# Interleaving the upper and lower halves of the weights column by column in one buffer

## The chip, the cores and the metric

The kernel runs on one core of one Trainium2 chip. The metric is the device time of one execution in microseconds (us). The core has five engines that run side by side and wait for each other through semaphores: TensorE (PE in the profile, with PEld for its weight loads), VectorE (DVE), ScalarE (ACT), GpSimd (POOL) and SyncE (SP, which issues the DMAs here). A matrix product on PE has two operands in SBUF: a stationary one of 128 x 128, which a weight load brings in, and a moving one, which a pass streams through the array. The result goes to PSUM. In the profile one pass is a MATMUL and the load ahead of it an LDWEIGHTS.

## The reference

Two pre-norm residual layers on x (256 tokens, 2,048 channels), float32 throughout:

```
h = rmsnorm(x, layer_norm[0]); y, gate = mla_mixer(h, ...)        # layer 0
x = x + (y * silu(gate)) @ mla_w_out
h = rmsnorm(x, layer_norm[1]); y, gate = swa_mixer(h, ...)        # layer 1
x = x + (y * silu(gate)) @ swa_w_out
return rmsnorm(x, final_norm)
```

Layer 0 is latent attention: h @ w_in gives a query latent and a key/value latent of 512 channels each, a rope key of 64 and a gate of 2,048; the latents are normed and projected up to 16 heads, and attention is causal. Layer 1 is sliding-window attention (window 128) with 32 query heads, 4 key/value heads and a sink logit per head. Almost all of the arithmetic is products of 256 tokens with weight matrices, 116 MB of weights in all.

## The kernel before

**Numbers in two halves.** A product in float32 is made of three passes in the format float32r. Each operand is split: `hi` is the value rounded to float32r, `lo` the rest. `proj` (lines 257 to 263) then adds hi x hi (line 261), hi x lo (262) and lo x hi (263) into one PSUM bank; in all three the weights (`wh`, `wl`) are stationary, 128 x 128, and the activations move, 128 x 256: `rhs[:, 0, :]` is their upper half, `rhs[:, 1, :]` their lower.

**Where the weights come from.** The class `Weights` keeps the list of all weight pieces, mostly 1,024 columns of 128 partitions, in the order of use. `load` fetches a piece by DMA into one of five raw buffers (`wraw`), three pieces ahead of the split. `split` makes the halves, two pieces ahead of use: ACT copies the piece into `whi` (line 93), DVE subtracts that from the raw piece into `wlo` (line 94). There are four pairs of such tiles, used in turn (`b` is 0 to 3), and `next` hands out a pair. One piece, the weights of the rope key (`w_kr`), goes through the other branch (lines 86 to 91), in which halves stand beside each other in blocks of 64 columns.

**Who uses them.** `slab` multiplies one piece of 1,024 columns with eight tiles of activations: 8 x 3 = 24 passes. Two slabs make 128 output channels. `hs0` to `hs15` are the normed input of a layer, `ys0` to `ys15` the gated output of the mixer, `cq` and `ck` the latents; each such tile has two halves of 256 columns (2,048 bytes a partition). Lines 530 to 532 (values of layer 0) and 613 to 615 (values of layer 1) are the other way round: activations are stationary and the weights move. Lines 738 and 745 do the last two output channels' blocks, with the lower halves of the weights first.

**Stages.** The input projection of layer 0 (16 pieces with eight banks open), eight groups of two heads, the output projection into x with 32 slabs on `ys`, the keys and values of layer 1, then 16 columns of sliding-window attention (loop over `c`: two slabs of query projection, two of gate, the scores of the next column, the products with the values), and the second output projection on `ys`. Within an engine the instructions run in the order in which a scheduler of the framework puts them; it follows the program's order and its own estimate of when operands come free. It also makes the waits, by the bytes that two instructions share, and the wait for a buffer by the tile: whoever writes a tile first in its next use waits for the last reader of its previous use.

**Where the tiles lie.** A tile of a pool lies behind the one that was made before. The four pairs of weight tiles have 4,160 and 4,096 bytes a partition, since `HI` puts 64 unused bytes ahead of each upper half. Taken modulo 256 bytes, the halves of pairs 0, 1, 2, 3 begin at 64, 128, 192 and 0 in the built program (both halves of a pair alike). `hs` begins at 0, `ys` at 0 and the latents at 32; `gap1` and `gap2` are tiles that nobody reads, which move what lies behind them.

Of the kernel before, what the change touches and what calls it, by code (L numbers as in the profile page):

```python
# [18 lines left out]
F32 = mybir.dt.float32  # L19
F32R = mybir.dt.float32r  # L20
# [5 lines left out]
P = 128  # L26
# [15 lines left out]
SUB = 1024  # L42
XQ = 4
WARM = 2

HI = [64, 64, 64, 64]
LO = [0, 0, 0, 0]
MASK_MLA = [(i + 16) % 32 for i in range(32)]
MASK_SWA = [i + 8 if i < 8 else i - 8 if i < 16 else i for i in range(32)]

# [1 line left out]
class Weights:  # L52
# [24 lines left out]
    def split(self, upto):  # L77
        while self.done < min(upto, len(self.pieces)):
            self.load(self.done + 1 + self.ahead_load)
            src, (_, n, beside) = self.raw.pop(self.done), self.pieces[self.done]  # L80
            self.done += 1
            b = (self.done - 1) % self.sub_bufs
            hi = self.pool.tile([P, SUB + HI[b] // 4], F32R, tag=f"whi{b}", name="whi", bufs=1)[:, HI[b] // 4:][:, 0:n]
            lo = self.pool.tile([P, SUB + LO[b] // 4], F32R, tag=f"wlo{b}", name="wlo", bufs=1)[:, LO[b] // 4:][:, 0:n]
            if beside:
                for i, t in enumerate((hi, lo)):
                    t = t.rearrange("p (k a c) -> p k a c", a=2, c=beside)
                    part = src[:, i * n // 2:(i + 1) * n // 2].rearrange("p (k c) -> p k c", c=beside)
                    self.nc.scalar.copy(out=t[:, :, 0, :], in_=part)
                    self.nc.vector.tensor_tensor(out=t[:, :, 1, :], in0=part, in1=t[:, :, 0, :].bitcast(F32),  # L90
                                                 op=ALU.subtract)
            else:
                self.nc.scalar.copy(out=hi, in_=src)  # L93
                self.nc.vector.tensor_tensor(out=lo, in0=src, in1=hi.bitcast(F32), op=ALU.subtract)  # L94
            self.ready.append((hi, lo))
# [8 lines left out]
def trunk(ctx: ExitStack, tc: tile.TileContext, a: dict):  # L104
# [3 lines left out]
    const = ctx.enter_context(tc.tile_pool(name="const", bufs=1))  # L108
# [9 lines left out]
    w = Weights(nc, wpool, raw_bufs=5, sub_bufs=4, ahead_load=3, ahead_split=2)  # L118
# [73 lines left out]


    hs = [const.tile([P, 2, S], F32R, name=f"hs{c}") for c in range(KC)]
    const.tile([P, 64], F32, name="gap1")
    ys = [const.tile([P, 2, S], F32R, name=f"ys{c}") for c in range(KC)]
    const.tile([P, 72], F32, name="gap2")


    def tiny(name, n=2, bufs=2):  # L200
# [196 lines left out]
    for k in range(KC):  # L397
        if k in (1, 3, 6):
            i = (1, 3, 6).index(k) + 1
# [6 lines left out]
        if k == 0:  # L406
            for half in range(2):
                hi, lo = w.next()
# [4 lines left out]
        elif k < KC - 2:  # L413
            hi, lo = w.next()
            for c in range(2 * RC):
                n = slice(c * P, (c + 1) * P)
                proj(acc[c], (hi[:, n], lo[:, n]), hs[k], False, False)
            sq_x.add(xc(k - 1))
        elif k == KC - 1:
# [3 lines left out]
            for c in range(2 * RC):  # L423
                n = slice(c * P, (c + 1) * P)
# [27 lines left out]
    def mix(g, vt, pt, sgs):  # L452

        (vh, vl, v1), (pth, ptl, pt1) = vt, pt
        yp = bank(ps_y, "yp")
        for j in range(2):
            v = slice(j * VD, (j + 1) * VD)
            n = slice(j * S, (j + 1) * S)
            o = yp[:, n]
            mm(o, lhsT=vh[:, v], rhs=pth[:, n], start=True, stop=False)  # L460
            mm(o, lhsT=vl[:, v], rhs=pth[:, n], start=False, stop=False)
            mm(o, lhsT=vh[:, v], rhs=ptl[:, n], start=False, stop=False)
            mm(o[:, P:], lhsT=v1[:, v], rhs=pt1[:, j * P:(j + 1) * P], start=False, stop=True)
        for j in range(2):
            n = slice(j * S, (j + 1) * S)
            yg = work.tile([P, S], F32, tag="yg", name="yg", bufs=2)
            dve.tensor_tensor(out=yg, in0=yp[:, n], in1=sgs[j], op=ALU.mult)
            split(ys[2 * g + j], yg)

    mixes = None  # L470
    for g in range(HEADS // 2):

        ps = bank(ps_p, "pp")
        hi, lo = w.next()
# [15 lines left out]
        if g == 0:  # L490
            t = bank(ps_y, "yp")
            tot = [q.total(t[:, 4 * i:4 * i + 4]) for i, q in enumerate((sq_x, sq_c["q"], sq_c["k"]))]
            r0 = rsqrt("r0", tot[0], D)

            sqc = rsqrt("sqc", tot[1], RANK, r0)
            nsq = small.tile([P, 2], F32, name="nsq")
            dve.tensor_tensor(out=nsq, in0=sqc, in1=r0, op=ALU.mult)
            dve.tensor_scalar(out=nsq, in0=nsq, scalar1=-MLA_SCALE, scalar2=None, op0=ALU.mult)
            skc = rsqrt("skc", tot[2], RANK, r0)
            sk = small.tile([P, 2], F32, name="sk")  # L500
            dve.tensor_tensor(out=sk, in0=skc, in1=r0, op=ALU.mult)
            t = bank(ps_y, "yp")
            r0B = row("r0B", r0, t[:, 0:S])
            skB = row("skB", sk, t[:, S:])
            ps = bank(ps_s, "sc")[:, 0:S]
            mm(ps, lhsT=fold, rhs=krn, start=True, stop=True)
            kr = work.tile([P, S], F32, tag="ro3", name="ro3")
            rope(kr, ps, cos0, sin0, MASK_MLA)
            dve.tensor_tensor(out=kr, in0=kr, in1=r0B, op=ALU.mult)
            split(krs, kr)  # L510

        ps = bank(ps_p, "pp")
        hi, lo = w.next()
# [10 lines left out]
        hi, lo = w.next()  # L524
        for i in range(2):
            t = slice(i * P, (i + 1) * P)
            for k in range(RC):
                n = slice(k * S, (k + 1) * S)
# [77 lines left out]
    for q in range(4):  # L606
        hi, lo = w.next()
        for i in range(2):
            t = slice(i * P, (i + 1) * P)
            for k in range(4):  # L610
                kk = 4 * q + k
                n = slice(k * S, (k + 1) * S)
# [79 lines left out]
    def gated(c):  # L692
        yg = work.tile([P, S], F32, tag="yg", name="yg", bufs=2)
        dve.tensor_tensor(out=yg, in0=y_of.pop(c), in1=sg_of.pop(c), op=ALU.mult)
        split(ys[c], yg)
# [37 lines left out]
    for c in tail:  # L733
        last[c] = [w.next(), w.next()]
        ps = bank(ps_p, "pp")[:, 0:S]
        for k in range(KC):
            n = slice(k % (KC // 2) * P, (k % (KC // 2) + 1) * P)
# [3 lines left out]
    def chunk(c, t):  # L741
        ps = bank(ps_p, "pp")[:, 0:S].rearrange("p (a q) -> p a q", a=2)
        for k in range(KC):
            n = slice(k % (KC // 2) * P, (k % (KC // 2) + 1) * P)
            mm(ps, lhsT=last[c][k // (KC // 2)][0][:, n], rhs=ys[k][:, :, t], start=k == 0, stop=k == KC - 1)  # L745
        xl = xc(c)[:, t]
        for n in range(2):
            dve.tensor_tensor(out=xl, in0=ps[:, n, :], in1=xl, op=ALU.add)
        sq = work.tile([P, P], F32, tag=("hx", "yg")[c % 2], name="sql", bufs=2)
        act.activation(out=sq, in_=xl, func=AF.Square)  # L750
        return sq
# [13 lines left out]
    def scaled(i, t, r2):  # L765
        r2B = bank(ps_s, "sc")[:, 0:P]
        mm(r2B, lhsT=r2[:, 0:1].to_broadcast([P, P]), rhs=ident, start=True, stop=True)
        r2B = r2B.rearrange("p (a q) -> p a q", a=1)
        for n in range(KC // XQ):
            for h in range(0, XQ, 2):  # L770
                o = x_t[n][:, h:h + 2, t]
                dve.tensor_tensor(out=o, in0=o, in1=r2B.to_broadcast([P, 2, P]), op=ALU.mult)  # L772
                if n == 0:
                    nc.sync.dma_start(out=a["out"][i, n][:, h:h + 2, :], in_=o)
            if n > 0:
                nc.sync.dma_start(out=a["out"][i, n], in_=x_t[n][:, :, t])
# [3 lines left out]
    sq = chunk(KC - 2, t1)  # L780
    r2 = norm(t0, parts)
    parts = [sq, chunk(KC - 1, t1)]
    const.tile([P, 120], F32, name="rest")
    scaled(0, t0, r2)
    scaled(1, t1, norm(t1, parts))

# [80 lines left out]
```

## Time and profile before

| | |
|---|---|
| median of 2 runs | 697.21 us (697.18 to 697.25) |
| the profiled execution: time, span | 696.82 us, 695.0 us |
| granted TensorE clock in it | 0.995 |
| PE, DVE, ACT, POOL busy | 681.6, 533.9, 428.0, 66.4 us |
| weight traffic | 117.00 MB, mean 168 GB/s |

The span runs from the first to the last instruction of the profiled execution. A pass is listed as 0.28 us long, but passes overlap in the pipeline: what counts is the time from the start of one to the start of the next. In a row of the groups, `pp<-hs,whi` names the output and the inputs, then come the shape, the count, the busy time and the mean length in ns of one, and behind the bar the idle time of the engine just before them and what ended it. The lines that the argument needs stand in the prediction.

### The profile page before, as it was taken

Reading aid. Unit: us, or ns where it says so; the run is one execution under the profiler, and the core shown is the slowest. Engines: PE = TensorE matmul, PEld = TensorE weight load, DVE = VectorE, ACT = ScalarE, POOL = GpSimd, SP = SyncE. Lnnn points to the kernel's source line nnn. Section 1 sums busy time; section 2 is a strip of 40 time slices with the busy share of each in tenths; the row PEclk is TensorE's granted clock in tenths of the full one; section 3 lists DMA queues with packets and bytes.
Section 4 is the critical chain, followed back from the end, with each engine's and each line's share of the span. In section 5 each row is a group of like instructions: output and inputs, shape, how many; then the busy total and the mean of one; then the engine's idle time right before and its main releaser. Section 6 shows DMA issues by size and latency. Waiting matters only on the chain.

```text
span 695.0 us, 14550 instructions
## 1 busy us (share of the span) xinstructions
PE 681.6 (98%) x5718; PEld 677.7 (98%) x5718; DVE 533.9 (77%) x1085; ACT 428.0 (62%) x853; POOL 66.4 (10%) x72
## 2 busy tenths in 40 slices
PE   8999999999999999999999999999999999999994
PEld 7999999999999999999999999999999999999994
DVE  5887787687688686666658899998998998766664
ACT  6666756666666665444446687687778768544430
POOL 3534000000000000111110000000000000022220
PEclk9999999999999999999999999999999999999998
DMA  8674554554554455555555544545445454455614
GB/s 311 243 223 143 167 164 139 170 166 142 174 164 144 162 174 162 193 182 190 182 183 171 165 156 152 171 149 162 157 149 165 152 168 153 153 185 187 191 45 122
DMA packets 37301, 117.00 MB, mean 168 GB/s; under 512 B 4208, under 2 KB 8944, under 8 KB 37232
## 3 DMA queue, kind: packets, MB, share of 16 engines
q1 hardware_dynamic: 37232, 116.06, 51.7%
q8 instruction: 45, 0.74, 0.4%
q14 instruction: 24, 0.20, 0.1%
HBM read 113.95 MB, written 2.10 MB: 167 GB/s over the span
## 4 chain that ended last, share of the span: by engine, by line
PE 89%; DVE 3%; ACT 3%; POOL 2%; issue 1%; DMA 1%; SPq 0%; DVEq 0%; ACTq 0%; POOLq 0%
PE pp L262 24%; PE pp L261 24%; PE pp L263 24%; PE pt L353 1%; ACT whi L93 1%; PE pp L745 1%; PE yp L680 1%; PE pp L532 1%; PE pp L530 1%; PE pp L531 1%; DMA wraw<-in_w_c 1%; DVE wlo L94 1%; POOL sq_x L227 1%; PE pt L354 1%; DVE x L772 1%
## 5 line engine op out<-in xcount | busy, mean ns | idle before, releaser
L93 ACT CAST whi<-wraw 128x1024 fp32r<-128x1024 f32 (+1 forms) x217 | 222.7, 1028 | 181.3 <-PE pp L262 155.7
L94 DVE TENSOR_TENSOR wlo<-wraw,whi 128x1024 fp32r<-128x1024 f32 (+1 forms) x217 | 259.9, 1199 | 92.8 <-ACT whi L93 91.7
L261 PE MATMUL pp<-hs,whi 128*128 128x256 f32 x860 | 243.0, 283 | 0.5 <-ACT whi L93 0.5
L263 PE MATMUL pp<-hs,wlo 128*128 128x256 f32 x860 | 242.4, 282 | 0.9 <-DVE wlo L94 0.9
L262 PE MATMUL pp<-hs,whi 128*128 128x256 f32 x860 | 242.1, 282 | 0.2 <-DVE hs L211 0.2
L261 PEld LDWEIGHTS pp<-hs,whi 128*128 128x128 f32 x860 | 163.1, 190 | 0.7 <-ACT whi L93 0.7
L263 PEld LDWEIGHTS pp<-hs,wlo 128*128 128x128 f32 x860 | 162.4, 189 | 1.4 <-DVE wlo L94 1.4
L262 PEld LDWEIGHTS pp<-hs,whi 128*128 128x128 f32 x860 | 162.5, 189 | 0.6 <-DVE hs L211 0.6
L261 PE MATMUL pp<-ys,whi 128*128 128x256 f32 x480 | 134.9, 281 | 0.0
L262 PE MATMUL pp<-ys,whi 128*128 128x256 f32 x480 | 134.9, 281 | 0.0
L263 PE MATMUL pp<-ys,wlo 128*128 128x256 f32 x480 | 134.7, 281 | 0.0
L227 POOL TENSOR_TENSOR sq_x<-sq_x,sq 128x256 f32<-128x256 f32 x43 | 53.4, 1242 | 589.4 <-ACT sq L226 343.2
L261 PEld LDWEIGHTS pp<-ys,whi 128*128 128x128 f32 x480 | 90.8, 189 | 0.0
L262 PEld LDWEIGHTS pp<-ys,whi 128*128 128x128 f32 x480 | 90.4, 188 | 0.2 <-DVE ys L206 0.2
L263 PEld LDWEIGHTS pp<-ys,wlo 128*128 128x128 f32 x480 | 90.5, 189 | 0.0
L339 ACT ACTIVATE p<-p,nm 128x128 f32<-128x128 f32 x96 | 42.7, 446 | 15.2 <-DVE nm L335 15.2
L261 PE MATMUL pp<-cq,whi 128*128 128x256 f32 x96 | 27.6, 287 | 0.0
L211 DVE SCALAR_TENSOR_TENSOR hs<-x,gains,hs 128x256 fp32r<-128x256 f32 x32 | 25.0, 792 | 2.8 <-ACT hs L210 2.8
L262 PE MATMUL pp<-cq,whi 128*128 128x256 f32 x96 | 27.0, 282 | 0.0
L263 PE MATMUL pp<-cq,wlo 128*128 128x256 f32 x96 | 27.0, 281 | 0.0
L314 DVE TENSOR_TENSOR qs<-ro,qs 64x256 fp32r<-64x256 f32 x48 | 20.2, 420 | 7.7 <-ACT qs L313 6.7
L313 ACT CAST qs<-ro 64x256 fp32r<-64x256 f32 x48 | 19.2, 400 | 8.2 <-DVE ro L307 7.6
(242 smaller groups left out, 1138.5 us busy)
## 6 DMA issues: line engine op xcount, KB each, us to landing
wraw<-in_w_g SPq DMA_DIRECT2D x64, 512.0 KB, 3.6
wraw<-in_w_o SPq DMA_DIRECT2D x64, 512.0 KB, 3.7
wraw<-in_w_q SPq DMA_DIRECT2D x32, 512.0 KB, 3.8
wraw<-in_w_ukv SPq DMA_DIRECT2D x16, 512.0 KB, 3.4
wraw<-in_w_c SPq DMA_DIRECT2D x15, 512.0 KB, 6.7
wraw<-in_w_uq SPq DMA_DIRECT2D x8, 512.0 KB, 3.8
wraw<-in_w_uq SPq DMA_DIRECT2D x8, 256.0 KB, 2.6
wraw<-in_w_k SPq DMA_DIRECT2D x4, 512.0 KB, 4.4
```

Source lines behind the costliest of these rows:

```text
L93: self.nc.scalar.copy(out=hi, in_=src)
L94: self.nc.vector.tensor_tensor(out=lo, in0=src, in1=hi.bitcast(F32), op=ALU.subtract)
L211: dve.scalar_tensor_tensor(out=dst[:, 1, :], in0=src, scalar=col, in1=dst[:, 0, :].bitcast(F32), op0=ALU.mult, op1=ALU.subtract)
L227: pool.tensor_tensor(out=self.acc, in0=self.acc, in1=t, op=ALU.add)
L261: mm(ps, lhsT=wh, rhs=rhs[:, 0, :], start=first, stop=False)
L262: mm(ps, lhsT=wh, rhs=rhs[:, 1, :], start=False, stop=False)
L263: mm(ps, lhsT=wl, rhs=rhs[:, 0, :], start=False, stop=last)
L313: act.copy(out=dst[r, j, :], in_=src[r, :])
L314: dve.tensor_tensor(out=dst[o, j, :], in0=src[r, :], in1=dst[r, j, :].bitcast(F32), op=ALU.subtract)
L339: act.activation(out=p[:, cols], in_=p[:, cols], func=AF.Exp, scale=-1.0, bias=nm[:, c:c + 1], accum_out=sm[:, c:c + 1])
L353: nc.tensor.transpose(t[:, 0, j * S + i * P:j * S + (i + 1) * P], p[:, i * P:(i + 1) * P], ident)
L354: nc.tensor.transpose(t[:, 1, j * P:(j + 1) * P], p[:, 2 * P:3 * P], ident)
```

## The change

The upper and the lower half of a piece now share one tile `w`, and their columns alternate: column n of `hi` is element 2n, column n of `lo` element 2n + 1. So 128 columns of either half span 1,024 bytes a partition where they spanned 512, and a pass of 256 columns of activations spans 1,024 as before. ACT writes every second element, DVE reads every second element of the tile and writes the ones between. Where the weights move (lines 530 to 532 and 613 to 615 of the kernel before), 256 columns span 2,048 bytes. The piece for the rope key keeps its halves apart, one behind the other in the shared tile.

```diff
-HI = [64, 64, 64, 64]
-LO = [0, 0, 0, 0]
+GAP = 64
...
             b = (self.done - 1) % self.sub_bufs
-            hi = self.pool.tile([P, SUB + HI[b] // 4], F32R, tag=f"whi{b}", name="whi", bufs=1)[:, HI[b] // 4:][:, 0:n]
-            lo = self.pool.tile([P, SUB + LO[b] // 4], F32R, tag=f"wlo{b}", name="wlo", bufs=1)[:, LO[b] // 4:][:, 0:n]
+            skip = GAP // 4 if b else 0
+            both = self.pool.tile([P, skip + 2 * SUB], F32R, tag=f"w{b}", name="w", bufs=1)[:, skip:skip + 2 * n]
             if beside:
+                hi, lo = both[:, 0:n], both[:, n:]
...
             else:
+                hi, lo = (both.rearrange("p (n a) -> p n a", a=2)[:, :, i] for i in range(2))
                 self.nc.scalar.copy(out=hi, in_=src)
                 self.nc.vector.tensor_tensor(out=lo, in0=src, in1=hi.bitcast(F32), op=ALU.subtract)
...
-    const.tile([P, 64], F32, name="gap1")
+    const.tile([P, 8], F32, name="gap1")
...
-    const.tile([P, 72], F32, name="gap2")
+    const.tile([P, 24], F32, name="gap2")
...
-    const.tile([P, 120], F32, name="rest")
+    const.tile([P, 224], F32, name="rest")
```

The three gaps add up to 256 columns before and after; they change what lies between. Modulo 256 bytes, the pairs 0, 1, 2, 3 now begin at 0, 64, 128 and 192 (the lower half 4 bytes on), `hs` at 0, `ys` at 32 and the latents at 128.

No instruction is added or taken away, and the code's order is the same. Because the two halves are one tile, the cast into a buffer now waits for the last pass that reads the lower half there, not for the last that reads the upper. The scheduler moves some instructions for that in the first groups and at the start of the sliding-window layer. In the columns of that layer the order on ACT is as before; this is one of them ahead of the change (`w...` are weight tiles, `fo` a part of the output, `ys_163` the gated output of the column, `pth` the transposed probabilities, `p` the scores; lines 339 and 663 are the softmax's exponentials, 344 and 345 its scaling):

```order
L685 COPY fo<-yp 64x256 x2
L93 CAST whi<-wraw 128x1024
L373 ACTIVATE th<-hx 128x256
L93 CAST whi<-wraw 128x1024
L205 CAST ys_163<-yg 128x256
L359 CAST pth<-pt 128x768
L93 CAST whi<-wraw 128x1024
L339 ACTIVATE p,sm<-p,nm 128x128
```

And this is the same column on ACT with the change:

```order
L687 COPY fo<-yp 64x256 x2
L95 CAST w<-wraw 128x1024
L375 ACTIVATE th<-hx 128x256
L95 CAST w<-wraw 128x1024
L207 CAST ys_163<-yg 128x256
L361 CAST pth<-pt 128x768
L95 CAST w<-wraw 128x1024
L341 ACTIVATE p,sm<-p,nm 128x128
```

Nothing moved there; line numbers are two higher.

## The prediction

> **What bounds the kernel now.** I read the page first, then busy time by stretches, then the groups by line, and last single passes in the timeline. The page:
>
> ```profile
> span 695.0 us, 14550 instructions
> PE 681.6 (98%) x5718; PEld 677.7 (98%) x5718; DVE 533.9 (77%) x1085; ACT 428.0 (62%) x853; POOL 66.4 (10%) x72
> PE 89%; DVE 3%; ACT 3%; POOL 2%; issue 1%; DMA 1%; SPq 0%; DVEq 0%; ACTq 0%; POOLq 0%
> ```
>
> TensorE is busy for 98% of the span and carries 89% of the chain that ended last, so time leaves this kernel only if the passes follow each other faster. How fast they follow now is read from the stretches:
>
> ```profile
> 200.00:300.00 100.00, 100.00 (x848) 100.00 (x848) 70.98 (x129) 58.91 (x112) 5.32 (x5) 1.00 0.52 169
> 400.00:500.00 100.00, 100.00 (x850) 100.00 (x850) 91.49 (x229) 77.31 (x182) 0.00 (x0) 1.00 0.49 159
> ```
>
> The columns are the stretch, then busy time and count of PE, PEld, DVE, ACT and POOL, the granted clock and the DMA share. A pass lasts 0.28 us in the records, so each count includes two or three passes that began earlier: 100 / (850 - 2.4) = 118.0 ns from one pass to the next, and 118.3 in the other stretch. The clock is full in both, and DVE is busy 91 us in one and 71 in the other, so neither the throttle nor the other engines' work sets that pace. The timeline shows what moves it:
>
> ```profile
> 301.78 0.28 PE L261 MATMUL pp<-ys,whi 128*128 128x256 f32 x1
> 303.20 0.28 PE L261 MATMUL pp<-ys,whi 128*128 128x256 f32 x1
> ...
> 299.98 0.28 PE L261 MATMUL pp<-ys,whi 128*128 128x256 f32 x1
> 301.42 0.28 PE L261 MATMUL pp<-ys,whi 128*128 128x256 f32 x1
> ...
> 611.78 0.28 PE L261 MATMUL pp<-ys,whi 128*128 128x256 f32 x1
> 613.36 0.28 PE L263 MATMUL pp<-ys,wlo 128*128 128x256 f32 x1
> ...
> 419.64 0.27 PE L354 MATMUL pt<-ident,p 128*128 128x128 f32 x1
> 419.97 0.27 PE L354 MATMUL pt<-ident,p 128*128 128x128 f32 x1
> ```
>
> Start to start, the first pair spans 12 passes in 1.42 us (118.3 ns), the second 12 in 1.44 us (120.0), the third 14 in 1.58 us (112.9). All are out-projection slabs: the same statements, the same shape, full clock, PE without a gap; counting pieces in the kernel gives weight buffers 0, 3 and 0 and tiles `ys0`, `ys8` and `ys4` onwards, so what differs is addresses. The last pair is three transposes, 0.33 us or 110 ns each: a pass of half the columns behind a load of the same 128 columns, so this is close to what a load takes alone. I conclude that a pass of 256 columns and the next load could both fit into about 110 ns, and that 3 to 10 ns more are lost because the two reads of SBUF get in each other's way at certain distances of their addresses. Now the pass covers 1,024 bytes a partition and the load beside it 512, so the distance drifts by 512 bytes within every pass and the bad distances come round each time.
>
> **The change part by part.** (a) The load. A column of `hi` now lies 8 bytes from the next, so the load covers 1,024 bytes and the distance stays what it was at the start; a stall shifts it, and then it stays shifted. Passes concerned:
>
> ```profile
> L261 PE MATMUL pp<-hs,whi 128*128 128x256 f32 x860 | 243.0, 283 | 0.5 <-ACT whi L93 0.5
> L261 PE MATMUL pp<-ys,whi 128*128 128x256 f32 x480 | 134.9, 281 | 0.0
> L261 PE MATMUL pp<-cq,whi 128*128 128x256 f32 x96 | 27.6, 287 | 0.0
> L261 PE MATMUL pp<-ck,whi 128*128 128x256 f32 x64 | 18.2, 284 | 0.0
> L261 PE MATMUL sc<-hs,whi 128*128 128x256 f32 x60 | 16.8, 281 | 0.0
> L738 PE MATMUL pp<-ys,wlo 128*128 128x256 f32 x32 | 4.0, 281 | 0.0
> L745 PE MATMUL pp<-ys,whi 128*128 128x256 f32 x64 | 8.0, 282 | 0.0
> ...
> 0.00:20.00 20.00, 17.29 (x114) 15.35 (x115) 12.12 (x18) 14.34 (x25) 7.10 (x22) 1.00 0.84 305
> ```
>
> Line 261 has 1,560 passes; 262 and 263 have as many, so 4,680. About 100 of the 114 in the first 20 us are such passes, but PE waits for data there; without them 4,580, and with 32 + 64 of lines 738 and 745 4,676 passes that set the time. (The key rope's weights, line 441, stay as they were.) The new pace is not in the trace. It is bounded by 113 ns, the best run of this shape that still drifts, and by 110 ns, the load alone. A price worse than 118 has no row and is a rival below. I take the middle, 111.5, because nothing drifts any more but the four buffers still begin at four distances (0, 64, 128, 192 bytes modulo 256 against `hs`, 32 less against `ys`), of which one may be poor. 4,676 x (118.0 - 111.5) ns = 30.4 us.
>
> (b) The splits. ACT (line 93) and DVE (line 94) now write at every second column, and DVE reads `hi` so. They are as many as before and none stands on the path, as the waits show:
>
> ```profile
> L94 DVE TENSOR_TENSOR wlo<-wraw,whi 128x1024 fp32r<-128x1024 f32 x207 | 253.0, 1224 | 87.8 <-ACT whi L93 87.2 <-PE pt L354 0.3
> L93 ACT CAST whi<-wraw 128x1024 fp32r<-128x1024 f32 x207 | 216.7, 1048 | 180.1 <-PE pp L262 155.7 <-issue 18.6 <-PE sc L615 2.0
> PE pp L263 <- DVE wlo L94: 0.9, 1, 0.9
> 413.20:426.65 13.45, 13.45 (x117) 13.45 (x116) 12.52 (x32) 10.43 (x26) 0.00 (x0) 1.00 0.47 157
> 480.44:493.88 13.44, 13.44 (x116) 13.44 (x116) 12.23 (x31) 10.21 (x25) 0.00 (x0) 1.00 0.47 158
> ```
>
> PE waits 0.9 us in all for the low halves. No row has a stride of two columns, so the price of one is bounded from 0 to a doubling (1.2 us for each split on DVE); I take 0, as the form, the type and the count stay. [...]
>
> (c) What is late next. The last two rows are columns of the sliding-window layer: 13.45 us of PE, with DVE busy 12.2 to 12.5 in them. A column has 96 of the passes of (a), so it would shrink by 96 x 6.5 ns = 0.62 us to 12.8, and DVE would be 96 to 98% full. Its order there stays as it was, and its waits for ACT no longer fit in free time. I give back 0.2 us in each of 14 columns: 2.8 us (between 0 and 14 x 0.6 = 8).
>
> (d) The wait of a buffer. `hi` and `lo` are now one tile, so the cast waits for the last pass on `lo` (line 263), not on `hi` (line 262): one pass, 0.12 us later. Behind it on ACT stand a softmax's exponentials, for which the transposes wait; but ACT waits for PE 155.7 us on line 93 now, with splits two pieces ahead of PE, so this costs 0. If ACT lost that lead, 0.12 us for each of 207 splits would be 25 us.
>
> (e) Weights as the moving side. Lines 530 to 532 and 613 to 615 stream the weights, at every second column now:
>
> ```profile
> L530 PE MATMUL pp<-whi,ck 128*128 128x256 f32 x64 | 18.2, 284 | 0.0
> L613 PE MATMUL sc<-whi,hs 128*128 128x256 f32 x32 | 9.1, 283 | 0.0
> ```
>
> 3 x 64 + 3 x 32 = 288 passes. The ends: 8 ns better each (-2.3 us), or twice as long (+34 us). I take 0, the pass's present length, and keep both ends. (f) The gaps only move addresses: 0 by themselves.
>
> Sum: 30.4 - 2.8 = 27.6 us less. The profiled execution took 696.8 us (span 695.0), the median of the runs is 697.2, so 696.8 - 27.6 = 669.2, put at 669.6 beside the median. With 113 ns it is 673.4 (no column is DVE's then), with 110 and nothing given back 659.4, and (e) may add to either: the likeliest case's own range is 656 to 682.
>
> **The rivals.** *No change.* The 118 ns may be mostly a fixed cost of handing from load to pass, and addresses only jiggle it. For it: 118.0 and 118.3 ns in stretches with different tiles. Against it: runs of 113 and 120. A mixture of good and bad distances among the four buffers ends here too: about 697, and 690 with half the buffers better by 3 ns. [...]
>
> *Slower by the load's span.* If the loss comes from the lines that the load touches, not from drift, 512 bytes cost 118.0 - 110 = 8 ns now and 1,024 would cost 16: 126 ns, +8 x 4,676 = 37.4 us, 735. It decides as soon as a strided load costs more than the 8 ns that there are to win. Against it: the load of 512 bytes in the best run costs 3 ns, in another 10, with the same number of lines. [...]
>
> *Slower by the splits.* If a stride of two makes DVE's split dearer by more than 0.25 us (20%), four splits fill the 1.0 us that DVE has left in a column; doubled, a column takes 12.4 + 4.9 = 17.3 us, +3.9 us x 16 = 62 us, 759. Nothing in the profile speaks for it; it is only unpriced.
>
> **How the numbers follow.** Likeliest case 0.66, no change 0.15, load's span 0.13, splits 0.06. Predicted is the likeliest's 669.6. The range that leaves out the two slow cases holds about 0.8: from 655 (110 ns, nothing given back, (e) helping) to 703 (669 with all of (e)'s 34 us, which also takes in no change). Two per cent, about what a measurement of this kernel can tell from no change, is 14 us: faster means under 683. That gives faster 0.66, same 0.15, slower 0.19.
>
> **What would show it.** Right: start to start in lines 261 to 263 falls to 110 to 113 ns in most runs, the count of passes in 100 us from 850 to some 895, splits stay at 1.22 and 1.05 us, and a sliding-window column takes 12.7 to 13.0 us with DVE over 95% busy. Wrong: a steady pace of 118 or more in some buffers (the distances matter, drift does not), near 126 in all (span), splits above 1.4 us, or passes of lines 530 to 532 at twice the pace of the rest.

## The result and the profile after

| | before | after |
|---|---|---|
| median of 2 runs each | 697.21 us (697.18 to 697.25) | 738.42 us (738.38 to 738.47) |
| span of the profiled execution | 695.0 us | 736.6 us |
| granted TensorE clock in it | 0.995 | 0.996 |

The kernel became slower: the ratio of the times is 1.0591, with a 95% interval of 1.0546 to 1.0637. The prediction was 669.6 us, with a range up to 703. The first lines of the page of the kernel after:

```profile
span 736.6 us, 14530 instructions
PE 724.2 (98%) x5718; PEld 713.6 (97%) x5718; DVE 536.9 (73%) x1085; ACT 447.6 (61%) x853; POOL 66.5 (9%) x72
PE 93%; ACT 2%; DVE 2%; DMA 1%; POOL 1%; issue 1%; SPq 0%; DVEq 0%; ACTq 0%
```

PE has the same 5,718 passes, is still busy for 98% of the span and carries even more of the chain that ended last. The clock is the same. So the passes themselves follow each other more slowly. Busy time by stretches of the kernel after, with the columns as before:

```profile
200.00:300.00 100.00, 100.00 (x770) 98.36 (x769) 67.90 (x136) 58.92 (x108) 0.00 (x0) 1.00 0.45 145
500.00:600.00 100.00, 100.00 (x839) 100.00 (x839) 90.42 (x235) 75.63 (x176) 0.00 (x0) 1.00 0.47 155
484.00:497.62 13.62, 13.62 (x117) 13.62 (x115) 12.27 (x32) 10.46 (x24) 0.00 (x0) 1.00 0.50 156
```

Two things are to be seen. Among the columns of the sliding-window layer, where no weights move (the second row), 100 us hold 839 passes in place of 850: 100 / (839 - 2.4) = 119.5 ns start to start, and one column, from its transposes to those of the next (the third row), takes 13.62 us in place of 13.45. That is about 1.3%, and would make some 9 us over the whole span, not 41. In the first row, among the groups of layer 0, there are 770 in place of 848, and PEld isn't full there, so the passes are what lasts longer. Which passes, the groups by line show (kernel after; `ck` and `hs` are activations):

```profile
L532 PE MATMUL pp<-w,ck 128*128 128x256 f32 x64 | 26.7, 418 | 0.0
L533 PE MATMUL pp<-w,ck 128*128 128x256 f32 x64 | 27.0, 422 | 0.0
L615 PE MATMUL sc<-w,hs 128*128 128x256 f32 x32 | 13.6, 424 | 0.0
L96 DVE TENSOR_TENSOR w<-wraw,w 128x1024 fp32r<-128x1024 f32 x207 | 252.8, 1223 | 98.5 <-ACT w L95 97.1
L95 ACT CAST w<-wraw 128x1024 fp32r<-128x1024 f32 x207 | 236.4, 1145 | 181.3 <-PE pp L265 150.1 <-issue 21.0 <-PE sc L617 4.5
```

The first three are the passes in which the weights are the moving side. Before, such a pass lasted 280 to 284 ns; now 418 to 424. The DVE split costs what it did (1,224 before, 1,223 now). The cast on ACT costs 97 ns more (1,048 before, 1,145 now), and ACT still waits 150 us for PE there, so that lies in idle time. Single passes of the kernel after in the timeline give the pace of both kinds:

```profile
100.00 0.42 PE L534 MATMUL pp<-w,ck 128*128 128x256 f32 x1
101.37 0.43 PE L534 MATMUL pp<-w,ck 128*128 128x256 f32 x1
...
540.07 0.28 PE L265 MATMUL pp<-hs,w 128*128 128x256 f32 x1
542.95 0.28 PE L265 MATMUL pp<-hs,w 128*128 128x256 f32 x1
```

The first pair spans 6 passes on moving weights in 1.37 us: 228 ns each. The second spans 24 ordinary passes in 2.88 us: 120.0 ns. There are 288 of the first kind, so 288 x (228 - 118) ns = 31.7 us of the 41.2 come from lines 532 to 534 and 615 to 617.

### The profile page after: what moved, and what is told of

The parts are those of the page before. It is cut to its first block, busy times and chain, and to the rows that moved or that the text cites. A ratio compares the mean times of both kernels' runs of the same rounds, so it can differ in the third digit from the quotient of the medians.

```text
span 736.6 us, 14530 instructions
## 1 busy us (share of the span) xinstructions
PE 724.2 (98%) x5718; PEld 713.6 (97%) x5718; DVE 536.9 (73%) x1085; ACT 447.6 (61%) x853; POOL 66.5 (9%) x72
## 4 chain that ended last, share of the span: by engine, by line
PE 93%; ACT 2%; DVE 2%; DMA 1%; POOL 1%; issue 1%; SPq 0%; DVEq 0%; ACTq 0%
PE pp L265 24%; PE pp L264 24%; PE pp L263 24%; PE pp L533 2%; PE pp L534 2%; PE pp L532 2%; PE pt L355 2%; PE pp L747 1%; ACT w L95 1%; PE yp L682 1%; PE sc L617 1%; PE sc L615 1%; PE sc L616 1%; DMA wraw<-in_w_c 1%; PE pt L356 1%; DVE x L774 1%
## 5 line engine op out<-in xcount | busy, mean ns | idle before, releaser
L95 ACT CAST w<-wraw 128x1024 fp32r<-128x1024 f32 (+1 forms) x217 | 243.0, 1123 | 183.1 <-PE pp L265 150.1
L96 DVE TENSOR_TENSOR w<-wraw,w 128x1024 fp32r<-128x1024 f32 (+1 forms) x217 | 259.8, 1199 | 104.8 <-ACT w L95 103.4
L263 PE MATMUL pp<-hs,w 128*128 128x256 f32 x860 | 245.2, 285 | 0.4 <-ACT w L95 0.4
L265 PE MATMUL pp<-hs,w 128*128 128x256 f32 x860 | 243.7, 284 | 1.0 <-DVE w L96 0.9
L264 PE MATMUL pp<-hs,w 128*128 128x256 f32 x860 | 243.6, 283 | 0.1
L265 PEld LDWEIGHTS pp<-hs,w 128*128 128x128 f32 x860 | 168.1, 196 | 1.6 <-DVE w L96 1.6
L264 PEld LDWEIGHTS pp<-hs,w 128*128 128x128 f32 x860 | 168.7, 196 | 0.6 <-DVE hs L213 0.3
L263 PEld LDWEIGHTS pp<-hs,w 128*128 128x128 f32 x860 | 168.2, 196 | 0.8 <-ACT w L95 0.6
L264 PE MATMUL pp<-ys,w 128*128 128x256 f32 x480 | 136.2, 284 | 0.1
L263 PE MATMUL pp<-ys,w 128*128 128x256 f32 x480 | 136.0, 284 | 0.0
L265 PE MATMUL pp<-ys,w 128*128 128x256 f32 x480 | 135.8, 283 | 0.0
L264 PEld LDWEIGHTS pp<-ys,w 128*128 128x128 f32 x480 | 94.6, 197 | 0.3 <-DVE ys L208 0.3
L265 PEld LDWEIGHTS pp<-ys,w 128*128 128x128 f32 x480 | 94.5, 197 | 0.0
L263 PEld LDWEIGHTS pp<-ys,w 128*128 128x128 f32 x480 | 94.3, 197 | 0.0
L263 PE MATMUL pp<-cq,w 128*128 128x256 f32 x96 | 27.7, 288 | 0.0
L265 PE MATMUL pp<-cq,w 128*128 128x256 f32 x96 | 27.1, 283 | 0.0
L264 PE MATMUL pp<-cq,w 128*128 128x256 f32 x96 | 27.1, 282 | 0.0
L533 PE MATMUL pp<-w,ck 128*128 128x256 f32 x64 | 27.0, 422 | 0.0
L534 PE MATMUL pp<-w,ck 128*128 128x256 f32 x64 | 27.0, 421 | 0.0
```

Of the source, the lines that this page charges most:

```text
L263: mm(ps, lhsT=wh, rhs=rhs[:, 0, :], start=first, stop=False)
L264: mm(ps, lhsT=wh, rhs=rhs[:, 1, :], start=False, stop=False)
L265: mm(ps, lhsT=wl, rhs=rhs[:, 0, :], start=False, stop=last)
L533: mm(o, lhsT=lat["k"][k][:, 0, t], rhs=lo[:, n], start=False, stop=False)
L534: mm(o, lhsT=lat["k"][k][:, 1, t], rhs=hi[:, n], start=False, stop=k == RC - 1)
```

## The experiments

The question after this was twofold: is it the stride of the moving side alone that costs 32 us, and what does a strided load do by itself, since the expected 30 us of gain didn't come?

**Taking the change apart.** In the first kernel the stationary weights alternate as in the change, but the pieces that move (the second half of each `w_ukv` piece and all of `w_v1`) lie with their halves side by side. A flag of `add` says which:

```diff
-        w.add(a["w_ukv"][g], 2048)
+        w.add(a["w_ukv"][g][:, 0:SUB], SUB)
+        w.add(a["w_ukv"][g][:, SUB:], SUB, apart=True)
...
-        w.add(a["w_v1"][c], D)
+        w.add(a["w_v1"][c], D, apart=True)
...
+                if apart:
+                    hi, lo = both[:, 0:n], both[:, n:]
+                else:
+                    hi, lo = (both.rearrange("p (n a) -> p n a", a=2)[:, :, i] for i in range(2))
```

> The changed kernel with one thing undone: the pieces that move through the array (values of both layers, 288 passes) keep their halves side by side; the stationary pieces stay interleaved. Theory (the moving side pays for the stride: 229 ns a pass against 118): 288 x 111 ns = 32 us come back, 706 us, and the value passes take 117 to 120 ns again. Rival (the load's span): the stationary loads lost it all, the time stays within 3 us of 738. Rival (splits, waits of the shared tile): the same, within 3 us of 738.

The second has `apart=True` as the default, so nothing alternates; the shared tile, its wait and the new gaps stay as in the change.

> The changed kernel with all halves side by side inside the shared tile: its buffers, gaps and waits, but no stride anywhere. Theory (only the strides cost): as before within 5 us, 692 to 702. Rival (the new distances or the shared tile's later release cost part of the 41 us): 705 or more.

The third is the second with `apart=False` for the pieces that move, so only these alternate.

> As the run without any stride, but with the value pieces alone interleaved (288 passes whose moving side steps over every second column). Theory: 32 us above the run without any stride, about 729, passes of the values at 229 ns. Rival (the load's span): within 3 us of the run without any stride.

| kernel | loads | moving weights | us | ratio to before (95%) |
|---|---|---|---|---|
| before | side by side | side by side | 696.92 | |
| e2 | side by side | side by side | 694.80 | 0.9974 (0.9963 to 0.9984) |
| e1 | alternating | side by side | 705.63 | 1.0128 (1.0113 to 1.0143) |
| e3 | side by side | alternating | 727.53 | 1.0441 (1.0425 to 1.0456) |
| after (beside a before of 697.21) | alternating | alternating | 738.42 | 1.0591 (1.0546 to 1.0637) |

The parts add up. The shared tile and the gaps without a stride are worth -2.1 us. The stride of the moving weights costs 727.53 - 694.80 = 32.7 us without strided loads, and 738.42 - 705.63 = 32.8 with them. The stride of the loads costs 705.63 - 694.80 = 10.8 us. The rows by line confirm who pays. Of the kernel e1:

```profile
L536 PE MATMUL pp<-w,ck 128*128 128x256 f32 x64 | 17.9, 280 | 0.0
L267 PE MATMUL pp<-hs,w 128*128 128x256 f32 x860 | 244.8, 285 | 0.8 <-ACT w L98 0.8
L98 ACT CAST w<-wraw 128x1024 fp32r<-128x1024 f32 x207 | 235.2, 1139 | 169.8 <-PE pp L269 156.1 <-issue 6.3 <-PE sc L621 2.0
```

And of e3:

```profile
L536 PE MATMUL pp<-w,ck 128*128 128x256 f32 x64 | 26.9, 421 | 0.0
L619 PE MATMUL sc<-w,hs 128*128 128x256 f32 x32 | 13.7, 427 | 0.0
```

The long passes go with the stride of the moving side and with nothing else. The costlier cast (1,139 ns) stays in e1, where 32.8 of the 41.2 us are gone, and PE waits for it 0.8 us in all there (the second of its rows): it isn't on the path. What the strided loads cost is seen in the stretches of e1:

```profile
200.00:300.00 100.00, 100.00 (x837) 100.00 (x836) 70.18 (x128) 61.21 (x110) 4.32 (x4) 1.00 0.51 166
400.00:500.00 100.00, 100.00 (x839) 99.96 (x838) 90.83 (x237) 78.07 (x180) 0.00 (x0) 1.00 0.46 153
```

In the same stretches of e2:

```profile
200.00:300.00 100.00, 100.00 (x851) 100.00 (x849) 71.36 (x129) 59.82 (x111) 5.28 (x5) 1.00 0.51 170
400.00:500.00 100.00, 100.00 (x856) 100.00 (x856) 91.89 (x230) 77.88 (x183) 0.00 (x0) 1.00 0.49 160
```

The mean of 838 passes means 119.7 ns, that of 853.5 means 117.5: 2.2 ns more, which over all 4,676 passes would be 10.3 us of the 10.8.

**The price by itself.** The fourth kernel only runs passes on weights taken as data, in chains of one kind each: loads beside short passes of 128 columns, weights as the moving side, and slabs (128-column loads, 256-column passes, as in `proj`) at 16 distances between the load's and the pass's addresses, 16 bytes apart. One of the operands lies as this says:

```diff
+        if kind == "side":
+            return [sta[:, off + i * 1024 + k * n:off + i * 1024 + (k + 1) * n] for i in range(2)]
+        v = sta[:, off:off + 2048]
+        if kind == "alternate":
+            v = v.rearrange("p (n a) -> p n a", a=2)
+            return [v[:, k * n:(k + 1) * n, i] for i in range(2)]
+        v = v.rearrange("p (n a c) -> p n a c", a=2, c=4)
+        return [v[:, k * n // 4:(k + 1) * n // 4, i, :] for i in range(2)]
```

The last kind, "fours", takes four columns and skips four: it spans as many bytes as alternating columns do, but the columns stand together in blocks of 16 bytes.

> No model is computed: only products of 48 passes each on weights as data, in one stretch, so the time means nothing; what counts is start to start. Loads alone (passes of 128 columns): 109 ns with halves side by side; alternating 109 if the load has full rate with two columns a 16-byte line, 118 or more if the stride slows the load itself. Moving 256 columns side by side 113 to 120 ns, alternating 213 to 230 by the theory. Moving 512 side by side 215, alternating 430 by the theory. Slabs at sixteen distances, 16 bytes apart: by the drift theory that the forecast rested on, alternating runs fall into some of 110 to 113 and some above 120, by distance; by the line theory they lie near 120 at all distances, a load of one column repeated is the cheapest (110), and every third and fourth column are dearer than alternating ones.

The timeline of this kernel; each row is a chain with its start, its length and its count. L118, L123 and L129 are loads side by side, alternating and on every fourth column, beside short passes; L135, L141, L147, L152 and L157 are moving weights: 256 columns side by side, alternating, in fours, 512 columns side by side, 512 alternating (of the last, the row holds the part up to 90 us). L113, L100 and L107 are slabs whose load reads one column 128 times, every third column, and every fourth; L179 is the pass behind them:

```profile
31.20 5.48 PE L118 MATMUL acc<-mov,sta 128*128 128x128 f32 x48
36.51 5.82 PE L123 MATMUL acc<-mov,sta 128*128 128x128 f32 x48
42.16 11.42 PE L129 MATMUL acc<-mov,sta 128*128 128x128 f32 x48
53.38 7.30 PE L135 MATMUL acc<-sta,mov 128*128 128x256 f32 x48
60.52 11.04 PE L141 MATMUL acc<-sta,mov 128*128 128x256 f32 x48
71.38 5.83 PE L147 MATMUL acc<-sta,mov 128*128 128x256 f32 x48
77.05 5.62 PE L152 MATMUL acc<-sta,mov 128*128 128x512 f32 x24
82.50 7.87 PE L157 MATMUL acc<-sta,mov 128*128 128x512 f32 x17
...
276.27 21.93 PE L113 MATMUL acc<-mov,sta 128*128 128x256 f32 x192
298.04 33.60 PE L100 MATMUL acc<-mov,sta 128*128 128x256 f32 x192
331.47 45.24 PE L107 MATMUL acc<-mov,sta 128*128 128x256 f32 x192
376.55 0.39 PE L179 MATMUL acc<-mov,sta 128*128 128x512 f32 x1
```

Where one chain follows another at once, the difference of the starts over the count is the pace: loads side by side (36.51 - 31.20) / 48 = 110.6 ns, alternating 5.65 / 48 = 117.7. The clock was lowered in a part of L129 and L135 (the last section shows it), so they aren't used for this; 256 moving columns side by side are known from the kernels, some 118 ns. Alternating they take 226.3 ns, in fours 5.67 / 48 = 118.1. Both spread 256 columns over 2,048 bytes; so the span isn't what set the time here. What the times follow is how many blocks of 16 bytes are touched: 128 by alternating columns, 64 by fours. Without a stride 512 columns also touch 128 blocks, and take 5.45 / 24 = 227.1 ns. And 512 alternating columns, 256 blocks, take (93.36 - 82.50) / 24 = 452.5 ns (93.36 is the start of the next chain, shown further down). So by these chains the moving side takes some 1.77 ns for each block (226.3 / 128, 227.1 / 128, 452.5 / 256), and 256 alternating columns took as long as 512 that stand together. The 16 bytes are an estimate from the chains of this kernel, with one size for both sides: in blocks of 32 bytes the fours would touch as many as alternating columns do, yet they take 118.1 and 226.3 ns, and in blocks of 8 bytes loads at steps of two, three and four would all touch 128, yet they take 117.7 ns and, as the loads below show, 174.1 and 234.8. No step other than two was run on the moving side: that blocks count and not the mere fact of a step rests on the fours here, and on the loads below, which were run at three steps.

The loads follow the same count. From start to start again, over 192 passes each: one column 113.4 ns (110 was expected), every third column 174.1, every fourth 234.8. A load of 128 columns touches 96 and 128 blocks in the last two: 1.81 and 1.83 ns each. By that price, as an estimate, the 64 blocks of an alternating load take 117, close to the 117.7 measured. The 32 blocks of a load side by side would take 59, so something else, which no run shows, sets its 110.6. With two columns in a block the load took 117.7 ns, a little more than the 113.4 of slabs whose load reads one column; the moving side took 226.3 with two and 118.1 with four.

The slabs at 16 distances show what is left to be won by addresses. L86 is a load side by side (at distance 0, then 64, then 192 bytes), L93 an alternating one (at 0, then 176), in the timeline of the same kernel:

```profile
93.36 5.94 PE L86 MATMUL acc<-mov,sta 128*128 128x256 f32 x48
115.91 5.84 PE L86 MATMUL acc<-mov,sta 128*128 128x256 f32 x50
161.51 5.72 PE L86 MATMUL acc<-mov,sta 128*128 128x256 f32 x49
184.03 5.92 PE L93 MATMUL acc<-mov,sta 128*128 128x256 f32 x48
247.38 6.15 PE L93 MATMUL acc<-mov,sta 128*128 128x256 f32 x49
```

The length less one pass's own 0.28 us, over the steps in the row (47 to 49; the row of 50 holds two passes of its neighbours), gives 120.4, 113.5 and 113.3 ns side by side, 120.0 and 122.3 alternating. The mean over all 16 distances, from the starts of the chains, is (184.03 - 93.36) / 768 = 118.1 ns for the load side by side and (276.27 - 184.03) / 768 = 120.1 for the alternating one; the load of one column took 113.4. So the distance does matter, 7 ns a pass between 0 and 192 bytes side by side, but in the mean a load on alternating columns takes 2 ns more. The drift theory, by which alternating loads would reach 110 to 113 ns at some distances and pass 120 at others, finds no support in 120.0, 122.3 and that mean.

**Distances in the kernel.** The next two have no stride; all weight halves lie at one distance from the activations (64 and 0 bytes beyond a multiple of 256), where the kernel before has a mixture. On top of e2:

```diff
-            skip = GAP // 4 if b else 0
+            skip = 0 if b else GAP // 4
...
-    const.tile([P, 8], F32, name="gap1")
+    const.tile([P, 64], F32, name="gap1")
...
-    const.tile([P, 24], F32, name="gap2")
+    const.tile([P, 64], F32, name="gap2")
...
-    const.tile([P, 224], F32, name="rest")
+    const.tile([P, 128], F32, name="rest")
```

(for distance 0, `skip = 0`).

> No stride; every weight half begins 64 bytes beyond a multiple of 256, every tile of activations at a multiple of 256 (the distance 64 at which the probe's runs took 113.4 ns a pass). If distance alone sets the pace: slabs at 113.4 ns, 4.6 ns x 4,676 = 21.5 us less than before, about 675. If what came before a run decides too (before, buffer 0 stood at 64 and ran at 113 in some slabs and at 118 in others): a mixture, 678 to 695.

> The same with all weight halves at multiples of 256, distance 0, where the probe's runs took 120.0 ns. If distance sets the pace: 120 ns in all slabs, 2 ns x 4,676 = 9 us more than before, about 706. If distance hardly matters in the full kernel: within 3 us of 695.

Distance 64 gave 683.46 us (ratio 0.9809, 0.9792 to 0.9825), distance 0 gave 704.63 (1.0109, 1.0094 to 1.0124). The order is as the probe said. At 0 the stretches from 200 to 300 and from 400 to 500 us hold 839 passes each, 119.5 ns, near the probe's 120.4. At 64, 113.4 ns throughout would have brought (117.5 - 113.4) x 4,676 = 19 us over e2; 11.3 came. The timeline of e5 shows why, in the first and the second output projection:

```profile
300.22 0.28 PE L266 MATMUL pp<-ys,w 128*128 128x256 f32 x1
303.05 0.28 PE L266 MATMUL pp<-ys,w 128*128 128x256 f32 x1
...
599.79 0.28 PE L266 MATMUL pp<-ys,w 128*128 128x256 f32 x1
602.51 0.28 PE L266 MATMUL pp<-ys,w 128*128 128x256 f32 x1
```

Each pair spans 24 passes: 2.83 us or 117.9 ns, then 2.72 us or 113.3 ns. Statements, shapes and distances modulo 256 bytes are the same; the pace is steady over all of both pairs. So one such distance had two paces here.

The last three: alternating loads at the good distance (e7, which is e1 with the lines above); everything at 192 (e8, `skip = 0 if b else 3 * GAP // 4`); and the upper halves at 64 with the lower at 192 (e9, with the gaps of e5, and the 32 columns between the halves in the rope key's branch too):

```diff
-            both = self.pool.tile([P, skip + 2 * SUB], F32R, tag=f"w{b}", name="w", bufs=1)[:, skip:skip + 2 * n]
+            skip = 0 if b else GAP // 4
+            both = self.pool.tile([P, skip + 2 * SUB + 64], F32R, tag=f"w{b}", name="w", bufs=1)[:, skip:]
...
+                    hi, lo = both[:, 0:n], both[:, n + 32:2 * n + 32]
```

> Stationary weights interleaved, value pieces side by side, and every weight tile at distance 64 from every tile of activations, the best distance without a stride (683.5 us there). If the load itself is what costs (117.8 ns alone in the probe, 120.1 in the mean over sixteen distances): no gain from the distance, 703 to 708 as with the change's own distances. If an interleaved load only needed a good distance: 685 or less.

> No stride, distance 192 instead of 64; the probe's runs took 113.4 ns at both. Slabs in either of two steady paces, 113.3 or 117.8 ns; if 192 falls into the first everywhere, 675, and as with 64 it is 683 to 684.

> No stride, upper halves at distance 64, lower at 192: in the same two paces, 675 to 690; it tells whether the step from upper to lower half decides which pace a slab falls into.

| kernel | us | ratio to before (95%) |
|---|---|---|
| before | 696.87 | |
| e7, alternating loads, all at 64 | 703.91 | 1.0099 (1.0084 to 1.0114) |
| e8, no stride, all at 192 | 689.97 | 0.9891 (0.9869 to 0.9912) |
| e9, no stride, upper at 64, lower at 192 | 675.20 | 0.9685 (0.9669 to 0.9701) |

With alternating loads the good distance wins 705.63 - 703.91 = 1.7 us, without them 694.80 - 683.46 = 11.3. That agrees with the probe, where the alternating load took 117.7 ns and a pass at its best 113.3 to 113.4. The time of e8 lies outside both values expected for it, 675 and 683 to 684. The kernel e9 beats both the kernel before and the one after. Its stretches:

```profile
200.00:300.00 100.00, 100.00 (x879) 100.00 (x878) 72.74 (x123) 60.78 (x109) 6.39 (x6) 1.00 0.54 176
400.00:500.00 100.00, 100.00 (x884) 100.00 (x883) 93.93 (x241) 80.52 (x188) 0.00 (x0) 1.00 0.51 165
```

And two passes of its first output projection in the timeline:

```profile
300.15 0.28 PE L266 MATMUL pp<-ys,w 128*128 128x256 f32 x1
302.87 0.28 PE L266 MATMUL pp<-ys,w 128*128 128x256 f32 x1
```

24 passes in 2.72 us are 113.3 ns, now in the stage where e5 had 117.9. By the counts the mean is 100 / (881.5 - 2.4) = 113.8 ns against some 118.1 before: 4.3 ns for 4,676 passes are 20 us, of the 21.7 won.

## Why the prediction was wrong, point by point

The forecast was 27.6 us less, and 41.2 more were measured. Two terms of the sum make the difference: (a) was put at -30.4 us and came out at +10.8, and (e) was put at 0 and cost 32.7.

**(a) The load, -30.4 us: wrong in sign.** The step that failed is the one from unequal spans to the loss: equal spans were to end a drift, and with it the loss. The measured term is +10.8 us (e1 less e2). Part of its base was right: PE does lose time where load and pass lie badly to each other: a pass took 119.5 ns in e6 (704.63 us) and 113.8 in e9 (675.20), and from 113.3 to 120.4 in the probe's slabs side by side, with the addresses alone changed. But e9 has 113.8 ns in the mean with spans of 512 and 1,024 bytes, as unequal as before, so drift isn't what costs. The reading of the rows before was too strong as well: those with 118.3 and 112.9 ns both have buffer 0 on `ys`, one distance modulo 256 bytes, so they didn't show that the distance alone decides; e5 has both paces at one distance again. And a load on alternating columns touches 64 blocks in place of 32 and takes 117.7 ns, where slabs whose load reads one column followed each other after 113.4. Two bounds failed with it. The lower one, 110 ns, was the load alone; a pass of 256 columns took 113.3 to 113.4 at its best, even with the load of one column. The upper one, 113, was the best run seen, so both ends lay on the side of a gain; "a price worse than 118 has no row" was no reason to leave it out of the bounds.

**(b) The splits, 0: right for the time.** DVE's price didn't change (1,223 ns). ACT's rose by 97 ns, inside the bounds, and is hidden in ACT's waits for PE, as predicted. The 0 was my choice between two ends, with no row of before behind it. DVE read and wrote every second column at its old price (1,224 to 1,223 ns), ACT's write there took 9% more (the 97 ns), and on the moving side of PE, for which (b) didn't ask, two columns to a block take 226.3 ns where four take 118.1.

**(c) DVE fills up, 2.8 us given back: not so.** In the change PE became slower and DVE had more room (12.27 of 13.62 us in a column). In e9, where PE comes near the pace that I had hoped for (113.3 ns against 111.5), DVE is busy 93.9 us of 100 and PE still 100: nothing is given back.

**(d) The later release, 0, and (f) the gaps, 0.** Together -2.1 us (e2 against before). So no lead was lost. But "the gaps only move addresses: 0 by themselves" was right only for these gaps: other gaps are worth up to 29 us between e6 and e9.

**(e) Weights as the moving side, taken as 0: the step that made most of the loss.** Its upper end, "twice as long (+34 us)", is what happened: 32.7 us. I had both ends and no row between them, and took the pass's present length, as if skipped columns were free on the moving side; no row of before said so. The range covered this end only on top of the gain of (a).

**The rivals.** "Slower by the load's span" gave 735 and the time is 738.4, but that is a coincidence. It had 126 ns for every load; the measured pace is about 120 (119.7 in e1), and nearly four fifths of the loss (32.7 of 41.2 us) come from 288 passes of which that rival doesn't speak. Its reason was nearer than mine, though: if its "lines" are the probe's 16-byte blocks, the load's time did rise with their number (110.6, 117.7, 174.1 and 234.8 ns for 32, 64, 96 and 128). "No change" and "slower by the splits" didn't come.

**What stays open.** Why one distance has two steady paces (113.3 and 117.9 ns in e5), what chooses between them, and why upper halves at 64 with lower at 192 hold the faster one where each distance for both halves gives a mixture (683.46 and 689.97). The runs of e8 spread from 687.54 to 690.35 us, so the choice may differ from one execution to the next; and weight buffers and activations that meet at one distance modulo 256 bytes still differ in their full addresses, which no run varied alone. The 113.3 ns that a pass of 256 columns took at its best is what its 64 blocks come to at the estimate of 1.77 ns (226.3 / 128); why a block takes that long isn't shown, nor why slabs with alternating loads took 120.1 ns in the mean, and 122.3 at one distance, where the load by itself took 117.7.

## What to carry to other kernels

Before a layout is changed, list everybody who reads it, and on which side: here 288 of 5,718 passes, those in which the weights move, made nearly four fifths of the loss. For float32r operands on PE the times here followed the 16-byte blocks that are touched, not the bytes that are spanned (256 moving columns over 2,048 bytes: 226.3 ns for 128 blocks, 118.1 for 64), so count blocks. Where two halves must share a buffer, whole halves side by side cost nothing here on either side (e2, 694.80 us against 696.92), and runs of four columns kept the pace on the moving side (118.1 ns); loads in runs of four weren't run. And before changing the form of an operand, try moving its start: 64 and 192 bytes in place of a mixture brought 3% here (675.20 us against 696.87), without an instruction more.

## What the runs showed of the hardware

On the moving side 64 blocks of 16 bytes took 118.1 ns, 128 took 226.3 and 227.1, and 256 took 452.5, some 1.77 ns a block by the longer ones; 256 float32r columns took 226.3 ns with every second one skipped and 118.1 in fours over the same bytes. A load of 128 columns took 110.6 ns on 32 blocks, and 117.7, 174.1 and 234.8 on 64, 96 and 128, some 1.83 ns a block from 64 on (an estimate from these three). ACT's write at every second column took 9% more (1,048 to 1,145 ns), DVE's read and write there no more (1,224 to 1,223 ns). One part of the fourth kernel ran under a lowered clock. Its stretches, two under the chain L129, two under L135 and one under L107:

```profile
42.20:46.10 3.90, 3.90 (x19) 3.90 (x18) 0.00 (x0) 0.00 (x0) 1.00 0.00 0
46.20:53.30 7.10, 7.10 (x32) 7.10 (x32) 0.00 (x0) 0.00 (x0) 0.50 0.00 0
53.40:56.30 2.90, 2.90 (x15) 2.90 (x15) 0.00 (x0) 0.00 (x0) 0.50 0.00 0
56.50:60.40 3.90, 3.90 (x35) 3.90 (x35) 0.00 (x0) 0.00 (x0) 1.00 0.01 4
331.00:377.00 46.00, 45.94 (x197) 45.62 (x196) 0.03 (x1) 0.00 (x0) 1.00 0.00 0
```

The columns are busy time and count of PE, PEld, ACT and POOL, then the granted clock. L129, loads on every fourth column, was under way when the clock fell from 1.00 to 0.50, and 0.50 holds in 7.10 of its 11.22 us; its passes start (53.38 - 42.16) us / 48 = 233.8 ns apart in the mean. L107, with the same kind of load beside longer passes, took 234.8 at full clock. So these loads didn't get slower with the clock. The passes of L135, 256 moving columns side by side, did: 15 passes are counted in 2.90 us at a clock of 0.50, and 35 in 3.90 us at 1.00, there 3.90 / (35 - 2.4) = 119.6 ns from one to the next.
